# Low-rank, gate and head-sum products from float32r halves, and VectorE block transposes in the triangular solve of an RWKV-7 branch

## Chip, cores and metric

The kernel runs on one core of a Trainium2 chip. The metric is the device time of one execution in microseconds. One execution is one launch of the whole program; the median of three executions is compared.

## What is computed

One decoder layer in inference, for 256 prompt tokens and for 8 sample sequences of 8 tokens (320 columns together), with d_model 2048. Three branches (HGRN2, RWKV-7, short gated convolution) read one wide projection; gates merge them, an output projection and an MLP with 8192 hidden channels follow. All arrays are float32. The part that matters here is the RWKV-7 branch:

```python
xs = rw + (prev - rw) * rw_mu                      # token shift of the projected rows
r, kr, vr, wd, ad, gd = jnp.split(xs, cuts, axis=-1)
w_log = -jax.nn.softplus(-(rw_w0 + jnp.tanh(wd) @ rw_w2)) - 0.5   # low-rank, 64 wide
decay = jnp.exp(-jnp.exp(w_log))
a = jax.nn.sigmoid(rw_a0 + ad @ rw_a2)             # low-rank, 64 wide
g = jax.nn.sigmoid(gd) @ rw_g2                     # gate, 128 wide
kk = hs(kr * rw_k_k)
kk = kk / jnp.maximum(jnp.sqrt(jnp.sum(kk * kk, -1, keepdims=True)), 1e-12)  # head sum
k = kr * (1.0 + (a - 1.0) * rw_k_a)
# per token: S = S (diag(w) - kk^T (a kk)) + v^T k ;  o = S r
bonus = jnp.sum(r_ * k_ * rw_r_k, -1, keepdims=True) * v_                    # head sum
o_rw = (groupnorm(o_rw) + bonus) * g
```

There are 16 heads of 64 channels; the recurrence starts from zero for the prompt and from given states for the samples.

## The kernel before

Channels lie on the 128 partitions and the 320 columns along the free dimension. Every dense product takes weight granules of 8 blocks of 128x128: SyncE's queue loads a granule (`raw`), ScalarE casts it to float32r (`whi_t`, L104), VectorE subtracts to get the low part (`wlo_t`, L105), each in two pieces of 512 columns; then TensorE runs three matmuls per block, high by high (L128), high by low (L129) and low by high (L130). High and low parts have three buffers each.

The stages run in this order. First the input is loaded, normalised and split (`xh`, `xl`, L199 and L200). Then comes `rwkv` with the short convolution in it: projections RWA and RG give the low-rank inputs `L` and `Lg`; then there are 8 pairs of heads, j = 0 to 7. For each pair, `rwkv_front(j)` makes three projections through `shift_mix` (k, r, v), the two low-rank products from `L` (L346, contraction over 64 rows each, one on the lower and one on the upper partitions), the head sum of the squared keys with the block matrix `bo1` (L368) and its reciprocal root, the scaled operands LYR and BK, the transposed values (L396, L397), the head sum for the bonus (L407), and the transposes of BK (L415). `rwkv_solve(j)` forms the products of each chunk of 64 tokens (L441 and after), inverts I - N: the 16x16 diagonal blocks go through DRAM to a layout with one block on a partition, where VectorE runs a back substitution of 15 steps (L472, L474), and come back through DRAM as `Pm` (L477); then two doubling steps, h = 16 and h = 32, each need M, the transpose of P: four TensorE transposes of 128x128 (L497), a ScalarE copy to `Mm` (L498), four products with N (L501), a masked copy (L504), four products with P (L507) and an addition (L508). `rwkv_chunks(j)` runs the four chunks in order, then the samples, group norm, and the gate product from `lg` and `Lg` (L609). Outside the float32r granules these products are float32; the profile shows each float32 matmul of L346, L368, L407 and L609 as two records, a transpose as one.

The source order in the loop is solve(j+1), chunks(j), short convolution, front(j+2). The tile framework orders each engine's instructions when the program is compiled, by priorities in source order, dependencies, free buffers and its own estimate of the durations; every engine then runs its list in that order and waits at semaphores. So granule matmuls of later projections stand between the small products. Most working tiles of a pair come from a pool with one buffer (`wp`); tiles with one tag share a buffer.

After that follow HGRN2 with the merge of the convolution branch, the other merges, the output projection and the MLP, which the change does not touch.

Of the kernel before, what the change touches and what calls it, by code (L numbers as in the profile page):

```python
# [9 lines left out]
F32 = mybir.dt.float32  # L10
F32R = mybir.dt.float32r
# [5 lines left out]
# Columns of every feature-major tile: 256 prompt tokens, then 8 sample  # L17
# sequences of 8 tokens each.
# [8 lines left out]
# Tile indices (128 columns each) inside w_in.  # L27
# [5 lines left out]
# Columns of the packed per-channel parameters.  # L33
# [10 lines left out]
# words between two diagonal 16x16 blocks of a [128, 640] array  # L44
# [5 lines left out]
def _constants():  # L50
    """Identity, block matrices and masks: they depend on shapes alone."""
    r = np.arange(128)
    s, q = r[:, None], np.arange(64)[None, :]
    c = np.arange(NT)
    cols = {}
    cols["id"] = np.eye(128)
    cols["bo1"] = (r[:, None] // 64 == r[None, :] // 64)
    cols["bo64"] = cols["bo1"] / 64.0
    up, upi = (s % 64 < q), (s % 64 <= q)
    same = (s % 64) // 8 == q // 8  # L60
    cols["mkp"] = np.concatenate([up, upi, up], 1)
    cols["mks"] = np.concatenate([up & same, upi & same, up & same], 1)
    first = np.where(c < NP, c % 64 == 0, c % 8 == 0)[None, :] & np.ones((128, 1), bool)
    cols["m01"] = ~first
    cols["m10"] = first
    cols["mb"] = (s % 64) // 8 == np.arange(8)[None, :]
    for h in _LV:
        n = np.arange(64 // h)[None, :]
        cols["left%d" % h] = (s // (2 * h) == n) & (s % (2 * h) < h)
        if h in (16, 32):  # L70
            cols["right%d" % h] = (s // (2 * h) == n) & (s % (2 * h) >= h)
    cols["eye16"] = np.broadcast_to(np.eye(16).reshape(1, 256), (128, 256))
    off, parts, o = {}, [], 0
    for k, v in cols.items():
        off[k] = (o, v.shape[1])
        parts.append(np.broadcast_to(v, (128, v.shape[1])).astype(np.float32))
        o += v.shape[1]
    return off, np.ascontiguousarray(np.concatenate(parts, 1))
# [8 lines left out]
class K:  # L87
# [19 lines left out]
    def granule(self, src, pool=None):  # L107
        """8 weight blocks of 128x128 as float32r high and low parts."""
        raw = self.wraw.tile([128, 1024], F32, name="raw")
        self.nc.sync.dma_start(raw, src)  # L110
        hi = (pool or self.whi).tile([128, 1024], F32R, name="whi_t")
        lo = (pool or self.wlo).tile([128, 1024], F32R, name="wlo_t")
        for q in range(2):
            c = slice(512 * q, 512 * q + 512)
            self.split(hi[:, c], lo[:, c], raw[:, c])
        return hi, lo

    def dense(self, granules, ah, al):
        """PSUM tile = sum over the granules of weight block ^T @ activation block."""
        ps = self.mm.tile([128, 512], F32, name="mm_t")  # L120
        n = len(granules) * 8
        i = 0
        for g in granules:
            hi, lo = self.granule(g)
            for k in range(8):
                w = slice(k * 128, k * 128 + 128)
                mmul = self.nc.tensor.matmul
                mmul(ps[:, :NT], hi[:, w], ah[:, i, :], start=(i == 0), stop=False)  # L128
                mmul(ps[:, :NT], hi[:, w], al[:, i, :], start=False, stop=False)  # L129
                mmul(ps[:, :NT], lo[:, w], ah[:, i, :], start=False, stop=(i == n - 1))  # L130
                i += 1
        return ps[:, :NT]

    def dense_wide(self, tiles, ah, al, psp, wpool):
        """Several column tiles at once, one activation block after the other."""
# [19 lines left out]
    def rsqrt(self, pool, v, tag):  # L155
        """1/sqrt(v): table square root, reciprocal, one Newton step."""
        nc = self.nc
        shp = [128, NT]
        y = pool.tile(shp, F32, name=tag + "_y")
        t = pool.tile(shp, F32, name=tag + "_t")  # L160
        nc.scalar.activation(t, v, AF.Sqrt)
        nc.vector.reciprocal(y, t)
        nc.gpsimd.tensor_mul(t, y, y)
        nc.gpsimd.tensor_mul(t, t, v)
        nc.vector.tensor_scalar(t, t, -0.5, 1.5, ALU.mult, ALU.add)
        nc.vector.tensor_mul(y, y, t)
        return y

    # -----------------------------------------------------------------------
    def build(self):  # L170
# [9 lines left out]
        self.onesr = cp.tile([128, 128], F32R, name="onesr")  # L180
        nc.sync.dma_start(self.p, io["par"])
# [7 lines left out]
        with ExitStack() as cx:  # L189
# [6 lines left out]
            nc.sync.dma_start(self.c, io["cst"])  # L196
            for k in range(KD):
# [14 lines left out]
        # operands of the sample sequences' new states wait in DRAM  # L212
# [40 lines left out]
    def shift_mix(self, wp, n, name, packed):  # L253
        """Projected tile n with the token shift mixed in; keeps the last rows."""
# [22 lines left out]
    def rwkv(self, cx):  # L277
# [16 lines left out]
        # tiles whose constant blocks are written once  # L294
# [10 lines left out]
        # DRAM scratch through which the diagonal 16x16 blocks change layout  # L305
# [7 lines left out]
        self.L = kp.tile([128, NT], F32, name="L")  # L313
        nc.scalar.activation(self.L[0:64, :], xwa[0:64, :], AF.Tanh)
        nc.scalar.copy(self.L[64:128, :], xwa[64:128, :])
        xg = self.shift_mix(w2, RG, "v", True)
        self.Lg = kp.tile([128, NT], F32, name="Lg")
        nc.scalar.activation(self.Lg, xg, AF.Sigmoid)
# [13 lines left out]

    def rwkv_front(self, j, wp, w2):
# [9 lines left out]
        # decay, gate and rate from the low-rank projections  # L343
        def lora(lhsT, rhs):
            ps = self.pa.tile([128, 512], F32, name="pa_t")
            T.matmul(ps[:, :NT], lhsT, rhs, start=True, stop=True)  # L346
# [5 lines left out]
        S.activation(sg, lora(lw[0:64, :], self.L[0:64, :]), AF.Sigmoid, bias=self.par("w0", j))  # L352
        S.activation(a, lora(lw[64:128, :], self.L[64:128, :]), AF.Sigmoid, bias=self.par("a0", j))
# [10 lines left out]
        # normalised kk, k with its rate  # L364
# [3 lines left out]
        T.matmul(ss[:, :NT], self.cst("bo1"), sq, start=True, stop=True)  # L368
# [22 lines left out]
        # token-major values: X holds [state or u ; v] per chunk and head  # L391
# [15 lines left out]
        T.matmul(bs[:, :NT], self.cst("bo1"), rk, start=True, stop=True)  # L407
        V.tensor_mul(vx, bs[:, :NT], vx)

        # token-major [beta ; kappa]  # L410
# [10 lines left out]
    def rwkv_solve(self, j, front, wp):  # L421
# [7 lines left out]
        # pairwise products inside each chunk  # L429
        Nb = Z["Nb"].rearrange("p (c w) -> p c w", w=128)  # L430
        GB = Z["GB%d" % (j % 2)].rearrange("p (c h w) -> p c h w", h=2, w=64)
        for mk, cc in (("mkp", slice(0, 4)), ("mks", slice(4, 5))):
# [10 lines left out]
            for h, rows in ((0, lo), (1, hi)):  # L443
                p3 = pp[h]
                orow = hi if h == 0 else lo
                ca = lo if h == 0 else hi        # columns of alpha
                cr = hi if h == 0 else lo        # columns of rho
# [9 lines left out]
        # P = (I - N)^-1: diagonal 16x16 blocks first, each on one partition  # L457
# [21 lines left out]
        # then doubling, with M = P^T  # L479
        Pm = Z["Pm%d" % (j % 2)].rearrange("p (c w) -> p c w", w=128)  # L480
        Mm = Z["Mm"].rearrange("p (c w) -> p c w", w=128)
        blk = lambda i: slice(i * 128, i * 128 + 128)
# [10 lines left out]
        for h in (16, 32):  # L493
            T3 = Z["T%d" % h].rearrange("p (c w) -> p c w", w=128)
            ps = self.pinv.tile([128, 512], F32, name="pi")
            for i in range(4):
                T.transpose(ps[:, blk(i)], Pm[:, i, :], ident)  # L497
            S.copy(Z["Mm"], ps)  # L498
# [12 lines left out]
    def rwkv_chunks(self, j, front, wp, w2):  # L511
# [13 lines left out]
        # prompt chunks in order  # L525
# [34 lines left out]
        # the sample sequences: all states against all tokens, then select  # L560
# [31 lines left out]
        # group norm per head, bonus, gate  # L592
# [16 lines left out]
        T.matmul(gp[:, :NT], lg, self.Lg, start=True, stop=True)  # L609
        V.tensor_mul(self.B[:, j, :], gp[:, :NT], o)  # L610

    def rwkv_state(self, j, wp):
        """New states of the sample sequences for one pair of heads."""
# [58 lines left out]
    def hgrn(self, cx, filler):  # L672
# [7 lines left out]
        # lower bound of the forget gate: softmax over the layers, its  # L680
        # cumulative sum less the first row, clipped
# [20 lines left out]
    def hgrn_head(self, j, w1, w2):  # L702
# [28 lines left out]
        # token-major values  # L731
# [9 lines left out]
        # A[s, t]: blocks (s0,t0) (s1,t1) (s0,t1) sample  # L741
# [17 lines left out]
        for h in (1, 2, 4, 8, 16, 32, 64, 128):  # L759
# [23 lines left out]
            # extend to blocks of 2h  # L783
# [13 lines left out]
        # outputs  # L797
# [10 lines left out]
        # states  # L808
# [16 lines left out]
        # norm over the head, gate  # L825
# [15 lines left out]
    def hgrn_load(self, heads, wp):  # L841
        """Operands of the sample sequences' new states, for two heads each:
        values per sequence, old states with their decay."""
# [114 lines left out]
    def norm_from(self, sp, pp, acc, tag):  # L958
        """Broadcast 1/sqrt(mean + eps): tokens on partitions for the scalar
        steps, then spread again by a product with a diagonal matrix."""  # L960
# [98 lines left out]
def _layout(a):  # L1059
# [3 lines left out]
    # weight granules: [column tile, half, row in block, block, column]  # L1063
# [58 lines left out]
```

## Time and profile before

| What | Value |
|---|---|
| Runs | 2499.78, 2500.53 and 2504.2 us, median 2500.53 us |
| Profiled execution | span 2502.3 us (the page gives no other time of its own); 42443 instructions |
| TensorE matmul busy | 2456.1 us, 98% |
| VectorE busy | 1523.7 us, 61% |
| ScalarE busy | 980.0 us, 39% |
| GpSimd busy | 409.4 us, 16% |
| Mean granted TensorE clock | 0.992 |

The span runs from the first to the last instruction of the profiled execution. Busy times of matmuls are modelled at their ends, and matmuls overlap in the pipeline, so the distance from one start to the next is what a matmul costs in a stream. The RWKV stage with the short convolution lies between about 30 us and 600 us of the span.

### The profile page before, as it was taken

The page shows a single profiled execution, that of the slowest core. Times are in us where ns is not written, and L with a number is a line of the kernel's source. Part 1 is how long each engine was busy: PE and PEld are TensorE (multiplying, and loading weights), DVE is VectorE, ACT ScalarE, POOL GpSimd, SP SyncE. Part 2 cuts the span into 40 slices and gives each one's busy share as a digit, 9 for nine tenths or more (in the row PEclk, how much of TensorE's full clock was granted, in tenths as well). Part 3 has the DMA queues.
Part 4 walks back from the last instruction along what each step waited for, and adds up shares of the span by engine and source line. Part 5 has one row for each costly group of instructions (what it writes and reads, how often), then busy time and mean ns, then how long its engine had stood idle before and what let it go on. Part 6 is the DMA issues. An engine that isn't in the chain of part 4 may idle for free.

```text
span 2502.3 us, 42443 instructions
## 1 busy us (share of the span) xinstructions
PE 2456.1 (98%) x16588; PEld 2337.3 (93%) x16588; DVE 1523.7 (61%) x3022; ACT 980.0 (39%) x1882; POOL 409.4 (16%) x558
## 2 busy tenths in 40 slices
PE   8999999999999999999999999899999999999998
PEld 7887888889999999999999897899999999999997
DVE  6878888786565665565555445854555555555555
ACT  5433434433433333343444334434333333333333
POOL 5423333231000000011111233400000000000003
PEclk9999999999999999999999999899999999999999
DMA  6333333334434344344444655444444444444443
GB/s 215 120 84 89 99 112 122 115 124 127 138 129 137 129 137 131 127 143 148 151 152 147 214 189 184 131 149 151 152 148 150 149 152 152 147 149 151 152 150 129
DMA packets 131703, 355.02 MB, mean 142 GB/s; under 512 B 34864, under 2 KB 43440, under 8 KB 131504
## 3 DMA queue, kind: packets, MB, share of 16 engines
q1 hardware_dynamic: 131504, 352.32, 43.1%
q8 instruction: 131, 2.15, 0.4%
q14 instruction: 68, 0.56, 0.1%
HBM read 337.13 MB, written 15.14 MB: 141 GB/s over the span
## 4 chain that ended last, share of the span: by engine, by line
PE 89%; DVE 7%; POOL 1%; DMA 1%; issue 1%; SPq 0%; ACT 0%; POOLq 0%; DVEq 0%; ACTq 0%
PE mm_t L128 27%; PE mm_t L129 26%; PE mm_t L130 26%; DVE wlo_t L105 1%; PE pi L501 1%; DMA Pm<-dP 1%; PE pi L441 1%; PE pho_t L805 1%; PE plv_t L765 1%; DVE x L941 1%; PE pi L507 1%; PE plv_t L766 0%; DVE hl L943 0%; DVE xl L200 0%; PE po_t L550 0%
## 5 line engine op out<-in xcount | busy, mean ns | idle before, releaser
L104 ACT CAST whi_t<-raw 128x512 fp32r<-128x512 f32 x1192 | 685.1, 619 | 1159.5 <-PE mm_t L129 726.5
L105 DVE TENSOR_TENSOR wlo_t<-raw,whi_t 128x512 fp32r<-128x512 f32 x1192 | 831.5, 727 | 304.2 <-ACT whi_t L104 295.4
L130 PE MATMUL mm_t<-xh,wlo_t 128*128 128x320 f32 x2080 | 656.1, 316 | 1.8 <-DVE wlo_t L105 1.7
L128 PE MATMUL mm_t<-xh,whi_t 128*128 128x320 f32 x2080 | 657.4, 316 | 0.0
L129 PE MATMUL mm_t<-xl,whi_t 128*128 128x320 f32 x2080 | 655.6, 315 | 0.0
L130 PEld LDWEIGHTS mm_t<-xh,wlo_t 128*128 128x128 f32 x2080 | 392.5, 189 | 9.1 <-DVE wlo_t L105 3.0
L128 PEld LDWEIGHTS mm_t<-xh,whi_t 128*128 128x128 f32 x2080 | 392.8, 189 | 8.0 <-issue 0.9
L129 PEld LDWEIGHTS mm_t<-xl,whi_t 128*128 128x128 f32 x2080 | 393.2, 189 | 4.6 <-issue 0.4
L128 PE MATMUL mm_t<-hh,whi_t 128*128 128x320 f32 x1232 | 382.2, 310 | 0.0
L129 PE MATMUL mm_t<-hl,whi_t 128*128 128x320 f32 x1232 | 381.4, 310 | 0.0
L130 PE MATMUL mm_t<-hh,wlo_t 128*128 128x320 f32 x1232 | 381.3, 310 | 0.0
L130 PE MATMUL mm_t<-rh,wlo_t 128*128 128x320 f32 x1024 | 316.8, 309 | 0.0
L128 PE MATMUL mm_t<-rh,whi_t 128*128 128x320 f32 x1024 | 316.8, 309 | 0.0
L129 PE MATMUL mm_t<-rl,whi_t 128*128 128x320 f32 x1024 | 316.8, 309 | 0.0
L128 PEld LDWEIGHTS mm_t<-hh,whi_t 128*128 128x128 f32 x1232 | 231.9, 188 | 6.5 <-ACT sqt L955 4.9
L129 PEld LDWEIGHTS mm_t<-hl,whi_t 128*128 128x128 f32 x1232 | 231.9, 188 | 0.0
L130 PEld LDWEIGHTS mm_t<-hh,wlo_t 128*128 128x128 f32 x1232 | 231.9, 188 | 0.0
L130 PEld LDWEIGHTS mm_t<-rh,wlo_t 128*128 128x128 f32 x1024 | 192.3, 188 | 0.0
L128 PEld LDWEIGHTS mm_t<-rh,whi_t 128*128 128x128 f32 x1024 | 192.3, 188 | 0.0
L129 PEld LDWEIGHTS mm_t<-rl,whi_t 128*128 128x128 f32 x1024 | 192.3, 188 | 0.0
L1024 DVE TENSOR_TENSOR m<-m,mm_t 128x320 f32<-128x320 f32 x112 | 54.7, 488 | 189.4 <-PE mm_t L130 189.4
L956 POOL TENSOR_TENSOR ssf<-ssf,sqt 128x320 f32<-128x320 f32 x14 | 13.9, 993 | 841.7 <-issue 809.6
(410 smaller groups left out, 2762.0 us busy)
## 6 DMA issues: line engine op xcount, KB each, us to landing
raw<-w_in SPq DMA_DIRECT2D x260, 512.0 KB
raw<-w_ff SPq DMA_DIRECT2D x256, 512.0 KB
raw<-w_o SPq DMA_DIRECT2D x32, 512.0 KB
hs<-s_hg SPq DMA_DIRECT2D x16, 512.0 KB
raw<-w_pc SPq DMA_DIRECT2D x16, 512.0 KB
raw<-w_pb SPq DMA_DIRECT2D x16, 512.0 KB
raw<-w_pa SPq DMA_DIRECT2D x16, 512.0 KB
o_hgs<-hsn SPq DMA_DIRECT2D x16, 256.0 KB
```

What stands on the lines that cost most here:

```text
L104: self.nc.scalar.copy(hi, src)
L105: self.nc.vector.tensor_sub(lo, src, hi)
L128: mmul(ps[:, :NT], hi[:, w], ah[:, i, :], start=(i == 0), stop=False)
L129: mmul(ps[:, :NT], hi[:, w], al[:, i, :], start=False, stop=False)
L130: mmul(ps[:, :NT], lo[:, w], ah[:, i, :], start=False, stop=(i == n - 1))
L441: T.matmul(pp[h][:, i, :], BK[rows, c, h:h + 2, :].rearrange("p a w -> p (a w)"), LYR[rows, c, h].rearrange("p a w -> p (a w)"), start=Tru ...
L501: T.matmul(ps[:, half(i)], Nb[:, i, :], cols(Mm[:, i, :], h, 0), start=True, stop=True)
L507: T.matmul(ps[:, half(i)], T3[:, i, :], cols(Pm[:, i, :], h, 1), start=True, stop=True)
L765: T.matmul(ps[:, 0:64], KS[:, 0:128], rh[:, 0:hb], start=True, stop=True)
L805: T.matmul(op[:, 256:320], s0[:, b, :], QX[:, 64 * b:64 * b + 64], start=(b == 0), stop=False)
L941: nc.vector.scalar_tensor_tensor(x1, t, self.par("g2", k), x1, ALU.mult, ALU.add)
L1024: nc.vector.tensor_add(d, d, ps)
```

## The change

The low-rank products, the gate product and the two head sums take float32r operands. A new helper `halves` splits a float32 tile into a float32r high and low part (one ScalarE cast, one VectorE subtraction). `three` makes a product of two split operands by three matmuls; `head_sums` multiplies the block matrix, held once in float32r as `bor`, with both halves of its operand by two matmuls. `L` and `Lg` become pairs of halves; `tanh` and `sigmoid` are written in place before. The halves take buffers of existing tags: those of the squared keys share `tk` and `rkk`, those of the bonus operand share `sq` and `rn_t`; the halves of `lw` and of `lg` share the new tags `lwh` and `lwl`. In the solve, the four TensorE transposes and the ScalarE copy of each doubling step become one VectorE transpose of 32x32 blocks over 128x512. `bor` is made by a VectorE copy that stands in the source ahead of the loop that splits the input. The remaining lines of the diff take out comments and docstrings.

```diff
+        self.bor = cp.tile([128, 128], F32R, name="bor")
...
             nc.sync.dma_start(self.c, io["cst"])
+            nc.vector.tensor_copy(self.bor, self.cst("bo1"))
             for k in range(KD):
...
-        self.L = kp.tile([128, NT], F32, name="L")
-        nc.scalar.activation(self.L[0:64, :], xwa[0:64, :], AF.Tanh)
-        nc.scalar.copy(self.L[64:128, :], xwa[64:128, :])
+        nc.scalar.activation(xwa[0:64, :], xwa[0:64, :], AF.Tanh)
+        self.L = self.halves(kp, xwa, NT, "L")
         xg = self.shift_mix(w2, RG, "v", True)
-        self.Lg = kp.tile([128, NT], F32, name="Lg")
-        nc.scalar.activation(self.Lg, xg, AF.Sigmoid)
+        nc.scalar.activation(xg, xg, AF.Sigmoid)
+        self.Lg = self.halves(kp, xg, NT, "Lg")
...
+    def halves(self, pool, src, n, name, tags=None):
+        h = pool.tile([128, n], F32R, name=name + "h", tag=tags[0] if tags else name + "h")
+        l = pool.tile([128, n], F32R, name=name + "l", tag=tags[1] if tags else name + "l")
+        self.split(h, l, src)
+        return h, l
+    def three(self, out, w, x, rows=slice(0, 128)):
+        mmul = self.nc.tensor.matmul
+        mmul(out, w[0][rows], x[0][rows], start=True, stop=False)
+        mmul(out, w[0][rows], x[1][rows], start=False, stop=False)
+        mmul(out, w[1][rows], x[0][rows], start=False, stop=True)
+    def head_sums(self, out, wp, src, tags):
+        h, l = self.halves(wp, src, NT, "hs", tags)
+        self.nc.tensor.matmul(out, self.bor, h, start=True, stop=False)
+        self.nc.tensor.matmul(out, self.bor, l, start=False, stop=True)
...
-        def lora(lhsT, rhs):
+        lwr = self.halves(wp, lw, 128, "lw", ("lwh", "lwl"))
+        def lora(rows):
             ps = self.pa.tile([128, 512], F32, name="pa_t")
-            T.matmul(ps[:, :NT], lhsT, rhs, start=True, stop=True)
+            self.three(ps[:, :NT], lwr, self.L, rows)
...
-        T.matmul(ss[:, :NT], self.cst("bo1"), sq, start=True, stop=True)
+        self.head_sums(ss[:, :NT], wp, sq, ("tk", "rkk"))
...
-        T.matmul(bs[:, :NT], self.cst("bo1"), rk, start=True, stop=True)
+        self.head_sums(bs[:, :NT], wp, rk, ("sq", "rn_t"))
...
         for h in (16, 32):
-            ps = self.pinv.tile([128, 512], F32, name="pi")
-            for i in range(4):
-                T.transpose(ps[:, blk(i)], Pm[:, i, :], ident)
-            S.copy(Z["Mm"], ps)
+            V.transpose(Z["Mm"], Z["Pm%d" % (j % 2)][:, 0:512])
...
-        T.matmul(gp[:, :NT], lg, self.Lg, start=True, stop=True)
+        self.three(gp[:, :NT], self.halves(wp, lg, 128, "lg", ("lwh", "lwl")), self.Lg)
```

More of the change, by code (lines that the diff above doesn't have):

```diff
@@ L351, in rwkv_front @@
         G.tensor_copy(wt[:, 0:1], self.zero)
-        S.activation(sg, lora(lw[0:64, :], self.L[0:64, :]), AF.Sigmoid, bias=self.par("w0", j))
-        S.activation(a, lora(lw[64:128, :], self.L[64:128, :]), AF.Sigmoid, bias=self.par("a0", j))
+        S.activation(sg, lora(slice(0, 64)), AF.Sigmoid, bias=self.par("w0", j))
+        S.activation(a, lora(slice(64, 128)), AF.Sigmoid, bias=self.par("a0", j))
         S.activation(wt[:, 1:], sg, AF.Exp, scale=-EXP_MHALF)
@@ L481, in rwkv_solve @@
         Mm = Z["Mm"].rearrange("p (c w) -> p c w", w=128)
-        blk = lambda i: slice(i * 128, i * 128 + 128)
         half = lambda i: slice(i * 64, i * 64 + 64)
```

## The prediction

> **What bounds the kernel now.** I read the page's busy times first, then the stretches by stage, then what TensorE waited for in the RWKV stage, then the timeline around each edited instruction.
>
> ```profile
> span 2502.3 us, 42443 instructions
> ...
> PE 2456.1 (98%) x16588; PEld 2337.3 (93%) x16588; DVE 1523.7 (61%) x3022; ACT 980.0 (39%) x1882; POOL 409.4 (16%) x558
> ```
>
> ```profile
> 62.00:130.00 68.00, 62.28 (x420) 58.72 (x421) 53.91 (x125) 30.10 (x62) 28.58 (x45) 0.95 0.39 121
> 130.00:600.00 470.00, 456.86 (x3241) 395.69 (x3240) 369.24 (x899) 181.19 (x376) 148.44 (x267) 0.99 0.34 104
> 600.00:1000.00 400.00, 399.90 (x2763) 390.40 (x2762) 245.80 (x564) 160.82 (x308) 37.67 (x43) 1.00 0.43 138
> ```
>
> Columns of the second: stretch, its length, busy time of PE, PEld, DVE, ACT and POOL, granted clock, DMA. TensorE bounds the whole; from 600 us it never rests. The change lies almost wholly in the RWKV stage, 62 to 600 us, where TensorE rests 5.7 + 13.1 = 18.9 us and VectorE is busy 53.91 + 369.24 = 423 of 538 us, 79% against 61% over the span. So what TensorE no longer does is time gained, unless VectorE, which gets new work, makes TensorE wait.
>
> ```profile
> PE pa_t L396 <- DVE xsv L271: 6.7, 3, 2.5
> PE pi L497 <- DMA Pm<-dP: 3.5, 3, 1.3
> PE pa_t L415 <- DVE t L472: 3.5, 1, 3.5
> PE pa_t L415 <- DVE BK L386: 1.8, 1, 1.8
> ```
>
> ```profile
> 100.00:105.00 5.00, 1.55 (x14) 1.31 (x13) 4.94 (x18) 1.60 (x3) 1.07 (x3) 0.96 0.00 0
> 104.00:112.00 8.00, 7.49 (x43) 7.07 (x44) 5.77 (x20) 3.10 (x10) 4.57 (x5) 0.57 0.34 80
> ...
> 292.00:296.00 4.00, 1.52 (x8) 0.84 (x6) 3.99 (x9) 0.00 (x0) 2.69 (x3) 0.97 0.17 6
> 295.00:300.00 5.00, 4.19 (x19) 3.87 (x20) 5.00 (x7) 2.46 (x7) 2.44 (x6) 0.66 0.12 9
> ```
>
> Above: who waited for whom in 60 to 600 us (total, times, longest). The long waits end on VectorE: three before the value transposes (L396), two before the BK transposes (L415). The stretches show two of these places: VectorE is busy 4.94 of 5 and 3.99 of 4 us while TensorE works 1.5 us. Behind each stands a lowered clock: 0.57 over 8 us loses 3.4 us, 0.66 over 5 us loses 1.7 us.
>
> **The change, part by part.** What a matmul costs in the stream is the distance of starts:
>
> ```profile
> 169.07 0.31 PE L129 MATMUL mm_t<-xl,whi_t 128*128 128x320 f32 x1
> 169.31 0.80 PE L346 MATMUL pa_t<-L,lw 64*128 64x320 f32 x2
> 170.04 0.41 PE L130 MATMUL mm_t<-xh,wlo_t 128*128 128x320 f32 x1
> 170.29 0.31 PE L128 MATMUL mm_t<-xh,whi_t 128*128 128x320 f32 x1
> ...
> 304.63 0.31 PE L129 MATMUL mm_t<-xl,whi_t 128*128 128x320 f32 x1
> 304.78 0.70 PE L407 MATMUL pa_t<-rkk,c 128*128 128x320 f32 x2
> 305.31 0.60 PE L497 MATMUL pi<-c,Pm 128*128 128x128 f32 x4
> 305.67 0.39 PE L130 MATMUL mm_t<-xh,wlo_t 128*128 128x320 f32 x1
> 305.90 0.31 PE L128 MATMUL mm_t<-xh,whi_t 128*128 128x320 f32 x1
> ...
> 357.15 0.81 PE L346 MATMUL pa_t<-L,lw 64*128 64x320 f32 x4
> 357.89 0.33 PE L534 MATMUL py_t<-X,LYR 128*64 128x64 f32 x3
> ```
>
> ```profile
> L346 PE MATMUL pa_t<-L,lw 64*128 64x320 f32 x32 | 10.4, 481 | 0.0
> ...
> L497 PE MATMUL pi<-c,Pm 128*128 128x128 f32 x64 | 10.4, 287 | 3.5 <-DMA Pm<-dP 3.5
> ...
> L407 PE MATMUL pa_t<-rkk,c 128*128 128x320 f32 x16 | 6.0, 455 | 0.9 <-DVE rkk L389 0.9
> L368 PE MATMUL pa_t<-sq,c 128*128 128x320 f32 x16 | 5.9, 451 | 0.1
> ...
> L609 PE MATMUL pa_t<-Lg,lg 128*128 128x320 f32 x16 | 5.6, 433 | 0.0
> ```
>
> A float32r matmul of 320 columns takes 0.15 us (304.63 to 304.78, 0.147 over a longer stream); a float32 product of two records takes 0.53 (304.78 to 305.31); four transposes take 0.36 and delay the next matmul by 0.08 more (0.23 instead of 0.15).
>
> *Transposes.* 64 records are 16 groups of four: 16 x 0.44 = 7.0 us leave TensorE. Nothing covers this, since TensorE is the bound. Ends: 5.8 (no delay behind) and, with the rest before L497 (3.5 us) gone as well, 10.5. I take 7.0: the DMA of Pm is not made earlier, so that rest moves to the products with N (L501).
>
> *Head sums.* 32 records are 16 products. Two float32r matmuls instead of one float32 product save 0.53 - 0.29 = 0.24. A matmul that waits for fresh halves may have its weight load exposed:
>
> ```profile
> L834 PE MATMUL plv_t<-sqh,onesr x8: 413/415/417, 647.1 to 1064.8; 128*128 128x320 f32 x8
> ...
> L835 PE MATMUL plv_t<-sql,onesr x8: 308/310/312, 647.8 to 1065.5; 128*128 128x320 f32 x8
> ```
>
> This is the same construct in HGRN2, the first line 0.105 us longer. Ends 0.13 and 0.24, taken in the middle: 16 x 0.18 = 2.9 us.
>
> *Gate product.* 0.53 becomes 3 x 0.147 = 0.44: 8 x 0.09 = 0.7 us. With two exposed loads the lower end is -0.9; `lg` is there early, so I take 0.7.
>
> *Low-rank products.* Two records cost 0.92: from 169.07 to 170.29 is 1.22, less two granule matmuls. Each of the two passes (0.27 in L407) carries about 0.1 more, and so do the neighbours: with 64 rows no weight load hides. Three float32r matmuls carry that three times: 3 x (0.147 + 0.10) + 0.19 at the neighbours = 0.93. So 0 gained, though the arithmetic alone says 0.09 each. Where loads hid, 16 x (0.92 - 0.44) = 7.7 would be gained. At 357.15 the two products of a pair run side by side (four records in 0.74); three of the eight pairs do so, and three matmuls in a row might not: up to 3 x 0.93 = 2.8 lost. I take 0, the value of the isolated row.
> The Trainium skill, "TensorE: Matmul & The Clock Gate", Part 3, says that a weight load overlaps running matmuls only when the row group differs. By that rule these products gain nothing, as the row has it; without it the sum would be better by 7.7.
>
> *New VectorE and ScalarE work.*
>
> ```profile
> L498 ACT COPY Mm<-pi 128x512 f32<-128x512 f32 x16 | 9.4, 586 | 26.9 <-PE pi L497 26.8
> ...
> L105 DVE TENSOR_TENSOR sql<-hsq,sqh 128x320 fp32r<-128x320 f32 x8 | 3.9, 492 | 40.0 <-ACT sqh L104 40.0
> ...
> L104 ACT CAST sqh<-hsq 128x320 fp32r<-128x320 f32 x8 | 3.7, 459 | 0.2
> ```
>
> ```profile
> L188 DVE CAST onesr<-ones x1: 292/292/292, 1.0 to 1.0; 128x128 fp32r<-128x128 f32 x1
> ```
>
> ```profile
> L105 DVE TENSOR_TENSOR wlo_t<-raw,whi_t 128x512 fp32r<-128x512 f32 x178 | 123.3, 712 | 8.5 <-ACT whi_t L104 7.5
> ```
>
> No block transpose is in the trace. Its nearest row has the same shape on the same engine, 0.71 us; ends 0.3 (the rate of the 128x128 cast on a quarter of the elements) and 1.42 (two passes). Per pair VectorE gets 2 x 0.71, two subtractions of 0.49 and two of 128x128 at about 0.29: 3.0 us. Over 8 pairs, with `L`, `Lg` and `bor`, that is 25 us, 79% becomes 83%. ScalarE swaps two copies of 0.586 for two casts of 0.459 and two small ones: nothing, and it is two thirds idle.
> Where TensorE's waits end on VectorE this work is not hidden. Ahead of the three L396 waits stand the subtractions of `lw` and the squared keys: 3 x 0.78 = 2.3 us. The two L415 waits, in the fronts with no earlier pair's work beside them, get cast and subtraction of the squared keys in the chain plus the one of `lw`: 2 x 1.24 = 2.5 us. Elsewhere granules split ahead cover it; with that cover gone at every pair, 8 x 3.0 = 24 us is the worst. Ends 0 and 24; I take 4.8, since only these five places show VectorE as the last to finish.
> The shared tags make `tk` wait for the head sum and the second halves for the root; both are in the same chain and not late elsewhere. The halves of `lw` wait for the gate product of an earlier pair, which needs little room, since its halves can be made when `lg` lands.
>
> *The wait for Pm.* It moves from TensorE to VectorE's list. Behind it stand weight splits; TensorE lives meanwhile on granules split ahead. 0 taken; if TensorE meets the 3.5 us twice, -3.5.
>
> *The copy to `bor`.*
>
> ```profile
> 6.98 13.55 DVE L200 SCALAR_TENSOR_TENSOR xl<-x,p,xh 128x320 fp32r<-128x320 f32 x16 [5.66 <-ACT xh L199]
> ```
>
> ```profile
> 13.64 0.39 ACT L468 COPY Pd<-c 40x256 f32<-40x256 f32 x1
> ```
>
> It joins VectorE's opening list, which is the chain before the first granule matmuls: 0.3 us. The constants were there by 13.64; placed after the eighth subtraction the copy waits for nothing.
>
> **Sum.** 7.0 + 2.9 + 0.7 + 0 = 10.6 off TensorE, 4.8 + 0.3 = 5.1 back: 5.5 us. The profiled span lies 1.8 us above the median of the runs, 2500.53; I subtract from the median: 2495.0 us.
>
> **Rivals.** *Cover holds everywhere.* Only averages matter: 17% of VectorE stays free, and the 4.8 does not appear. For it: from 300 to 600 us hardly a wait on VectorE is seen, and every list is ordered anew. Gain 10.3: 2490.2, or less if a lowered clock goes too.
> *VectorE takes the gain back.* The waits above double (12 us instead of 6.7 + 3.5 + 1.8), or `bor` is put at the head of the list and holds the splits from 6.98 to 13.64, 6.7 us: about 10.6 - 10 = 0.6 gained, 2500.
> *Slower: a new long wait with a lowered clock.* One mechanism: 3 us more VectorE work in a pair makes one wait like that at 292 us (2.5 us), and the clock falls behind it (3.4 us as at 104). Each costs 5.9. Two eat the 10.6; three give 17.7 - 10.6 = 7.1 slower, 2507.6. Against it: TensorE gets less work in a pair too, 1.3 us.
> The Trainium skill, same page, Part 1, puts the gate's window at 3.4 us, free-running, so that shorter waits need not lower the clock. The trace has it lowered behind a wait of 2.5 us, too; by the page's rule the rival would need longer waits than I priced.
>
> **How the numbers follow.** The forecast, 3 to 8 us gained, has 0.45; full cover 0.24; gain taken back 0.17; slower 0.14. A measurement tells 0.2%, 5 us, from no change. Of the forecast's 0.45, 0.28 lies beyond 5 us: faster 0.28 + 0.24 = 0.52, same 0.17 + 0.17 = 0.34, slower 0.14. The range goes from 2487 (full cover, with one lowered clock of 3.4 gone) to 2505, halfway into the slower case; its forecast alone spans 2492 to 2498.
>
> **What would show it.** L497 and the copy to Mm gone, a VectorE transpose of 0.6 to 0.8 us sixteen times; head sums at 0.29 to 0.40 from start to start; three low-rank records in about 0.9; VectorE at 83% from 62 to 600 us; the stage's end earlier by the whole gain, nothing after it. Wrong would be: TensorE's rest in the stage well above 24 us or below 19, more or fewer stretches of lowered clock, transposes above 1.4 us, low-rank products at 0.45, or a first granule matmul later than before.

## The result, and the profile after

The changed kernel takes 2534.13 us (median of 4 runs, 2533.97 to 2535.69) against 2501.81 us before: ratio 1.0128, 95% interval 1.0114 to 1.0143. It is 32 us slower; the forecast was 2495.0 us, range 2487 to 2505.

The head of the page of after:

```profile
span 2532.2 us, 42457 instructions
...
PE 2468.3 (97%) x16548; PEld 2356.5 (93%) x16548; DVE 1537.5 (61%) x3073; ACT 980.9 (39%) x1898; POOL 411.1 (16%) x558
```

The span is 29.9 us longer, yet TensorE has 40 records fewer and its busy time grew by 12. Matmuls that take longer without being more mean a lower clock. The stretches of after (columns as in the prediction: stretch, length, PE, PEld, DVE, ACT, POOL, clock, DMA) say where:

```profile
62.00:130.00 68.00, 57.85 (x390) 54.43 (x389) 54.06 (x129) 29.73 (x62) 27.72 (x45) 0.90 0.35 112
130.00:600.00 470.00, 442.29 (x3000) 391.34 (x2999) 364.14 (x901) 171.82 (x368) 146.22 (x255) 0.92 0.31 100
600.00:1000.00 400.00, 399.75 (x2765) 386.69 (x2764) 246.50 (x556) 159.62 (x307) 41.91 (x52) 1.00 0.39 135
```

From 130 to 600 us the granted clock is 0.92 instead of 0.99, TensorE rests 27.7 us instead of 13.1, and it starts 241 matmuls fewer. From 600 us on all is as before. The last product into `pa_t` starts at 622.1 us instead of 592.1, so the whole loss lies in the RWKV stage. Who waited for whom there (60 to 600 us: total, times, longest):

```profile
PE pa_t L351 <- ACT hsh L104: 11.7, 6, 4.9
PE pi L521 <- DVE Mm L518: 9.0, 6, 3.7
PE mm_t L128 <- DVE sh L671: 3.3, 2, 3.1
PE pa_t L351 <- DVE B L630: 2.4, 1, 2.4
```

None of these was among the long waits of before. The second, closely: TensorE, then VectorE (start, duration, what; in brackets the idle time before it and its releaser).

```profile
180.38 0.31 PE L129 MATMUL mm_t<-xl,whi_t 128*128 128x320 f32 x1
184.38 1.97 PE L521 MATMUL pi<-Mm,Nb 128*128 128x64 f32 x8 [3.69 <-DVE Mm L518]
186.86 1.97 PE L527 MATMUL pi<-Pm,T 128*128 128x64 f32 x8 [0.52 <-DVE T L524]
188.59 0.61 PE L351 MATMUL pa_t<-hsh,bor 128*128 128x320 f32 x1
```

```profile
175.61 2.14 DVE L385 RECIPROCAL Wi<-W 128x320 f32<-128x320 f32 x1
177.67 2.09 DVE L162 RECIPROCAL rn_y<-rn_t 128x320 f32<-128x320 f32 x1
...
180.68 1.14 DVE L406 TENSOR_TENSOR tk<-tk,xsk 128x320 f32<-128x320 f32 x1
...
183.61 0.71 DVE L518 STREAM_TRANSPOSE Mm<-Pm 128x512 f32<-128x512 f32 x1
```

The transpose itself takes 0.71 us, but it stands behind two reciprocals and much other work of the next pair's front, and TensorE has nothing but the solve next in its list: no granule matmul stands between L521 and L527. What happened to the clock (stretches of 3.4 us, TensorE alone: length, busy time, records, clock), first all matmuls, then the granule matmuls alone:

```profile
180.00:183.40 3.40, 0.69 (x5) 1.00 0.37 82
```

```profile
183.60:187.00 3.40, 2.11 (x9) 0.50 0.00 0
190.40:193.80 3.40, 3.40 (x17) 0.50 0.35 126
197.30:200.70 3.40, 3.40 (x18) 0.50 0.02 5
204.10:207.50 3.40, 3.40 (x12) 0.50 0.11 42
214.30:217.70 3.40, 3.40 (x19) 0.50 0.19 72
217.70:221.10 3.40, 3.40 (x27) 0.99 0.40 154
```

```profile
190.40:193.80 3.40, 0.27 (x1) 0.50 0.35 126
197.30:200.70 3.40, 0.00 (x0) 0.50 0.02 5
204.10:207.50 3.40, 2.52 (x9) 0.50 0.11 42
214.30:217.70 3.40, 2.50 (x9) 0.50 0.19 72
```

The clock fell after 3.4 us with 0.69 us of work, and then stayed at 0.50 for 34.1 us, though by the trace TensorE was busy without a gap from 190.4 to 207.5 us: at first with products of 64 columns and hardly a granule. It came back only after granule matmuls had filled more than half of four stretches in a row. The Trainium skill, "TensorE: Matmul & The Clock Gate", Part 1, has the clock fall after an idle window of about 3.4 us and return after one busy window of that length. The fall comes near this; the return does not, since 17 busy us did not bring it. What decides is not settled here: nine granule matmuls stand in the stretch at 204.10 as in that at 214.30.

### The profile page after: what moved, and what is told of

Read it like the earlier page. It is cut to its first block, busy times and chain, and to the rows that moved or that the text cites. A ratio compares the mean times of both kernels' runs of the same rounds, so it can differ in the third digit from the quotient of the medians.

```text
span 2532.2 us, 42457 instructions
## 1 busy us (share of the span) xinstructions
PE 2468.3 (97%) x16548; PEld 2356.5 (93%) x16548; DVE 1537.5 (61%) x3073; ACT 980.9 (39%) x1898; POOL 411.1 (16%) x558
## 4 chain that ended last, share of the span: by engine, by line
PE 88%; DVE 8%; POOL 2%; DMA 1%; issue 1%; ACT 0%; SPq 0%; DVEq 0%; POOLq 0%; ACTq 0%
PE mm_t L128 26%; PE mm_t L129 26%; PE mm_t L130 26%; DVE wlo_t L105 1%; PE pi L464 1%; PE pi L521 1%; PE pi L527 1%; DMA Pm<-dP 1%; PE pho_t L825 1%; PE plv_t L785 1%; DVE x L961 1%; PE plv_t L786 0%; DVE rn_y L162 0%; DVE hl L963 0%; DVE xl L202 0%
```

## The experiments

Times at the lowered clock below are summed from the trace's clock records up to 640 us: 17.1 us before, 92.2 after. Each kernel has one trace; those of e6 and e8 are of the shortest of four executions (2513.3 and 2525.9 us, medians 2518.07 and 2535.15). "Stage end" is the start of the last product into `pa_t`: 592.1 before, 622.1 after. Comparisons are with runs of before on the same chip, medians 2502.6 to 2502.9.

Theories at the start: T, the transposes in VectorE's list are late and TensorE waits; H, the split head sums make waits; later L (as T, with the clock falling where only small products follow), W (less TensorE work lowers the clock) and S (what loses is the new order of all lists, which the tile framework makes when it compiles; it is called the planner here).

**Which part.** e1 is before with this edit alone, e2 is after with it undone.

```diff
-            ps = self.pinv.tile([128, 512], F32, name="pi")
-            for i in range(4):
-                T.transpose(ps[:, blk(i)], Pm[:, i, :], ident)
-            S.copy(Z["Mm"], ps)
+            V.transpose(Z["Mm"], Z["Pm%d" % (j % 2)][:, 0:512])
```

> Kernel before with one part of the change: the solve's transposes by VectorE, all products as before. Theory T (the transposes stand in VectorE's list behind other work, TensorE's products with N wait for them up to 4 us and the clock falls behind those waits): slower than before by 12 to 25 us, 2514 to 2527, with most of the stretches of lowered clock of the changed kernel. Theory H (the split head sums make the waits): this part alone takes 7 us off TensorE and gives little back, 2494 to 2499. Rival S (every change of the list moves waits about, whichever part): anything, with waits at places that neither part touches.

> Changed kernel with the transposes back on TensorE and the copy to Mm on ScalarE; all products from float32r halves. Theory T: near before or faster, 2494 to 2503, since 4 us leave TensorE and the waits for Mm are gone. Theory H: slower than before by 12 to 25 us, 2514 to 2527, with TensorE waiting 10 us or more for the cast of the bonus operand (hsh). If both parts cost, each loses 10 to 20 us.

e1: 2530.53 us, ratio 1.0113 (1.0096 to 1.013), 81.9 us at the lowered clock. e2: 2521.76 us, 1.0073 (1.0058 to 1.0088), 61.4 us. Each part loses alone, e1 3 us beyond T's range, e2 within H's. But 28 + 19 is more than 32, so something common may be counted twice. In e1 the head sums are untouched and the longest wait is T's:

```profile
PE pi L498 <- DVE Mm L495: 11.5, 7, 2.5
```

**The halves' buffers, and the bonus sum.** e3 and e4 are after with one line changed:

```diff
-        self.head_sums(bs[:, :NT], wp, rk, ("sq", "rn_t"))
+        self.head_sums(bs[:, :NT], wp, rk, ("sg", "wt"))                          # e3
+        T.matmul(bs[:, :NT], self.cst("bo1"), rk, start=True, stop=True)          # e4
```

> Changed kernel, but the halves of the bonus operand take the buffers of sg and wt, which come free after the scan, instead of sq and rn_t, which come free only after the reciprocal root. If the shared buffers make the bonus head sum late, TensorE's wait for hsh (11.7 us in the changed kernel) falls under 4 us and the time to 2505 to 2520. If not, 2530 to 2537 and the wait stays.

> Changed kernel with the bonus head sum as one float32 product again; the rest as changed. Theory H: the wait for hsh and its lowered clock go, 2508 to 2520. Theory T: 2530 to 2538, since the waits for Mm stay (and 0.24 us per pair go back to TensorE).

e3: 2530.86 us, 1.011 (1.0095 to 1.0125). e4: 2532.95 us, 1.0123 (1.0107 to 1.0138). Neither is the cause; the waits only changed place. In e3 the wait for `hsh` (L351) falls from 11.7 to 4.6 us, and the one for the second half (L352) becomes 5.0. In e4 the head sum's is no longer among the longest, and the solve's has grown from 9.0:

```profile
PE pi L521 <- DVE Mm L518: 12.6, 8, 4.7
```

**Edits that change no work.** e5 moves the copy to Mm to VectorE (`V.tensor_copy`), e6 swaps the two low-rank lines of the source, e6b puts the three lines of the bonus product behind the BK transposes. All are made in the kernel before.

```diff
-            S.copy(Z["Mm"], ps)
+            V.tensor_copy(Z["Mm"], ps)                                     # e5
...
-        S.activation(sg, lora(lw[0:64, :], self.L[0:64, :]), AF.Sigmoid, bias=self.par("w0", j))
         S.activation(a, lora(lw[64:128, :], self.L[64:128, :]), AF.Sigmoid, bias=self.par("a0", j))
+        S.activation(sg, lora(lw[0:64, :], self.L[0:64, :]), AF.Sigmoid, bias=self.par("w0", j))   # e6
```

> Kernel before, with the copy of the transposes to Mm done by VectorE instead of ScalarE; all TensorE work as before. Theory L (a step of the solve that stands in VectorE's list comes late, TensorE waits for it in front of the small products of the solve, the clock falls there and stays low through them): slower by 10 to 25 us, 2512 to 2528, with waits of the products with N (L501) for a VectorE Mm and 50 us or more at the low clock before 640 us, against 17 in the kernel before. Theory W (the loss comes from the transposes being gone from TensorE's work): as before, 2499 to 2506.

> Kernel before with the two low-rank products in the other source order: the same instructions, another order of the lists. Rival S (the list of the kernel before is a lucky one and any other order loses): slower by 8 to 25 us, 2511 to 2528, with 40 to 80 us at the low clock before 640 us. Theory L: within 5 us of before, 2498 to 2508.

> Kernel before with the bonus head sum behind the BK transposes in the source: the same instructions, another order of the lists. Rival S: slower by 8 to 25 us, 2511 to 2528. Theory L: within 5 us of before, 2498 to 2508.

e5: 2518.89 us, 1.0064 (1.0049 to 1.0079), 44.4 us at the lowered clock. e6: 2518.07 us, 1.0066 (1.0042 to 1.0089), 34.1 us. e6b: 2522.23 us, 1.0079 (1.0064 to 1.0094), 54.6 us. e6 and e6b run the very instructions of before in another order and lose 16 and 20 us. So S is real, though e6's time at the lowered clock lies below S's 40 to 80 us, and the loss of e2 is no larger than that of a neutral edit. e5's time lies in L's range, but not by L's mechanism: no product with N (L501) waits for `Mm` there, and the longest wait is that of the bonus head sum:

```profile
PE pa_t L407 <- DVE rkk L389: 6.1, 3, 3.5
```

**Is it the missing TensorE work?** e8: before with Mm from the VectorE transpose, while TensorE still makes its four transposes into a tile that nobody reads.

```diff
-            S.copy(Z["Mm"], ps)
+            V.transpose(Z["Mm"], Z["Pm%d" % (j % 2)][:, 0:512])
```

> Kernel before with Mm made by VectorE's block transpose, while TensorE still makes its four transposes per step, whose result is not read. Theory L: as slow as with the transposes gone, 2525 to 2540, since Mm still stands in VectorE's list (and 7 us of TensorE work are kept). Theory W: as before, 2499 to 2508, since TensorE's work keeps the clock up.

e8: 2535.15 us, 1.013 (1.0114 to 1.0147). W falls: TensorE has all its work, and the loss is as large as that of the whole change. L has the time right and the wait wrong: TensorE waits only 2.1 us for `Mm` (L501), and 6.8 us for Pm to land ahead of the transposes that nobody reads.

All nine kernels to which the planner gave a new order (after, e1 to e6b, e8) lose, by 15 to 33 us.

**The order held.** The remaining kernels fix the order of every engine's list. At the end of the build each instruction is told to issue behind the one that precedes it in a stored list, without a wait. `traced` are the instructions in the order of the program's text, `at` is the next place of one engine's list.

```diff
+    info = mybir.DependencyInfo(mybir.DependencyClass.NoSync, mybir.DependencyReason.DATA)
...
+            at += d + 1
+            if last is not None:
+                tc.add_manual_dep(traced[at], traced[last].name, info, reason="order")
+            last = at
```

In the order of before, the edit's new instructions stand where the operand was ready in the profile of before, and products stand where the replaced ones stood.

> The kernel before with the solve's transposes on VectorE, and every engine's list held in the order of the kernel before (issue order only, no added wait): nothing moves but the 64 TensorE transposes and 16 ScalarE copies that go, and the 16 VectorE transposes, each put ahead of the first VectorE instruction that started after the first of its four TensorE transposes in the profile of before. If the loss comes from new orders (theory S), the clock's lowered time before 640 us stays near the 17.1 us of before (below 30), and the time is 2490 to 2502: the 7 us that the transposes' TensorE time was worth, less up to a VectorE instruction's wait (0.7 to 2 us) at a few of the 16. If a transpose in VectorE's list is late wherever it stands (theory T, L), TensorE waits 2 to 4 us ahead of L521 in some of the 16 steps, over 40 us run at the lowered clock and the time is 2512 or more, about the 12 us by which the kernels with VectorE transposes lay above those without.

e9: 2503.73 us, 1.0004 (0.9995 to 1.0013), 27.3 us at the lowered clock, stage end 593.7. The 27 us that e1 loses beyond this are order, which includes the places of the transposes in VectorE's list. But nothing is gained either: the time is 1.7 us above S's range and even with before. From 62 to 620 us (columns as above), before and e9:

```profile
62.00:620.00 558.00, 539.04 (x3792) 474.04 (x3793) 440.97 (x1066) 223.34 (x462) 182.42 (x318) 0.98 0.36 109
```

```profile
62.00:620.00 558.00, 533.53 (x3716) 468.81 (x3715) 447.15 (x1079) 213.65 (x443) 180.82 (x317) 0.98 0.36 108
```

TensorE works 5.5 us less and rests 5.5 us more. Most of the new rest has one address, in place of the 3.5 us before L497; the bonus head sum's wait (L407) grows from 0.9 to 2.2 us:

```profile
PE pi L498 <- DVE Mm L495: 6.7, 6, 3.3
```

**The halves with the order held.** For the bonus sum the shared tags `sq` and `rn_t` exclude before's order (there the bonus product comes ahead of the root of the squared keys), so it stays float32; the halves of `lg` share the tag `YA` and have one of their own.

> The float32r halves alone (low-rank, gate and squared-key head sum; the bonus head sum stays float32, since its shared buffers would forbid the order), with TensorE's transposes, every list in the order of the kernel before; the new casts and subtractions stand where their source was ready in the profile of before. Theory S: 2496 to 2502, since nothing moves and the products save 8 x 0.18 (head sums), 8 x 0.09 (gate) and 16 x 0.09 (low-rank) = 3.6 us at most. Theory H (the extra casts and subtractions ahead of the products make waits of themselves): 2510 or more, as the 2521.8 us of the halves in their own order.

> The whole change but the bonus head sum, every list in the order of the kernel before. Theory S: the gains of the two add up, 2486 to 2500 us, faster than before, against 2532.95 us for the same instructions in the order that the planner gave them: then all of the loss is order. Theories T, L: 2512 or more, with over 40 us at the lowered clock before 640 us.

e10: 2519.55 us, 1.0066 (1.0053 to 1.008). e11: 2517.84 us, 1.0065 (1.0051 to 1.008). What ran is not what the text expected: by an error in the stored list, most low-rank matmuls stood where the head sum belonged, so `a` came late:

```profile
PE pa_t L351 <- ACT a L376: 9.7, 3, 3.4
```

By accident they show that misplacing some 40 matmuls costs 9 to 13 us, against the next two kernels, which have the lists as intended.

> e10 with its mistake mended: halves for low-rank, gate and squared-key head sum at the places of the products that they replace, transposes on TensorE. S: 2496 to 2503 (nothing moves, up to 3.6 us of TensorE time saved, a few tenths of waits for the new casts). H: 2510 or more, near the 2521.8 us of the halves in the planner's order.

> In e10 and e11 the order was not held: five of the six low-rank matmuls of each tile had been put where the squared-key head sum stood in TensorE's list, so the second sigmoid came some 6 us late and TensorE waited for it. Here each group of three, and each pair of halves, stands exactly where the float32 product that it replaces stood; else as e11 (whole change but the bonus head sum, every other list in the order of the kernel before). Order theory S: 2495 to 2503, that is the 2503.7 us of the transposes alone in this order less up to 3.6 us for the products, against 2532.95 us in the planner's order. If the halves cost by themselves (H): 2510 or more.

e13 (halves): 2506.8 us, 1.0016 (1.0007 to 1.0025), clock as before (17.1 us). e12 (both): 2508.38 us, 1.0021 (1.0013 to 1.003), 37.5 us. Both lie 4 to 5 us above S's bounds, and 3 and 2 us below H's. e4 has e12's instructions, but for the buffers of `lg`, in the planner's order: 2532.95 - 2508.38 = 24.6 us are order. What is left against before, 5.8 us, is again waits; in e13 the one before the value transposes has grown from 6.7 us and three times to

```profile
PE pa_t L419 <- DVE xsv L273: 9.5, 4, 3.1
```

VectorE begins the `xsv` of the three places of before 0.5, 1.1 and 2.0 us later. The subtractions that now stand ahead of it may be why; no run takes them out.

**The mirror.** Every instruction of before in the order that the planner gave e1, the TensorE transposes up to eight granule matmuls ahead of their use.

> The mirror: the instructions of the kernel before, every one, in the order that the planner gave the kernel with VectorE transposes (e1); the four TensorE transposes stand up to 8 matmuls ahead of the products that need them, the ScalarE copy where the VectorE transpose had run. S: the order alone makes the loss, 2520 to 2540, with over 50 us at the lowered clock before 640 us, though no instruction is changed. If the transposes on VectorE, not the order, make the extra loss over a neutral reordering: 2515 to 2521, like the swapped low-rank products (2518.1).

e14: 2539.07 us, 1.0142 (1.0119 to 1.0165). No instruction of before is changed, and 36.5 us are lost, no less than in e1. The intervals of the two overlap, so the 2539.07 - 2530.53 = 8.5 us between them are not a measure of the transposes. The waits moved to the landing of Pm and the ScalarE copy:

```profile
PE pi L497 <- DMA Pm<-dP: 10.0, 4, 3.1
PE pi L501 <- ACT Mm L498: 5.9, 7, 1.7
```

The first stands ahead of the TensorE transposes, whose places were chosen for this kernel and not by the planner; part of e14's loss may be theirs. e6 and e6b have no such choice in them.

What the two orders differ in can be read from the built lists. Granule matmuls between the four products with N and the four with P, for the 16 doubling steps:

```text
before 8 5  2 7  3 4  7 3  11 6  4 13  1 7  5 9     none: 0 of 16
after  9 5  0 4  0 3 14 5   2 5  5 14  0 4  7 5     none: 3
e1     7 5  0 0  0 0  6 0   1 4  3  1  1 2  5 7     none: 5
e14    7 5  0 0  0 0  6 0   1 4  3  1  1 2  5 7     none: 5
```

Where nothing stands between, TensorE waits for VectorE's masked copy (0.52 us before L527 above), and only 64-column products run. This goes with the longest stretches at half clock: in the ten traces with a new order (e14's among them), 11 of the 12 stretches of over 20 us hold such a step, and the kernels in before's order have neither. But 16 of the 31 such steps lie outside these stretches, so a step of this kind does not always bring one, and no run changed the granules between these products alone.

**Two tries at a version faster than before.** e15 is e12 with this; e16: before in its own order, with three groups of value transposes moved behind the next 13, 10 and 17 granule matmuls; e17: e9 with the same moves.

```diff
+            if j < 6:
                 V.transpose(Z["Mm"], Z["Pm%d" % (j % 2)][:, 0:512])
+            else:
+                ps = self.pinv.tile([128, 512], F32, name="pi")
+                for i in range(4):
+                    T.transpose(ps[:, i * 128:i * 128 + 128], Pm[:, i, :], ident)
+                S.copy(Z["Mm"], ps)
```

> A version to beat both: as e12, but VectorE transposes only for tiles j below 6; the last two tiles, where e9 showed waits of 3.3 and 1.7 us ahead of L498, keep TensorE's. S: 2503.7 less 5.0 for those waits, 3.4 for the lowered clock at 492.9 us, 3.6 for the halves, plus 4 x 0.57 for the transposes that stay: 2494, range 2489 to 2500. If the halves cost by themselves: above 2505.

> The kernel before, its own order held, but for three places in TensorE's list: the three vx transposes (L396, L397) of tiles 2, 3 and 4 stand 13, 10 and 17 granule matmuls later (0.147 us each), so that these fill the waits of 1.92, 2.31 and 2.48 us for xsv that the profile of before shows at 176.6, 237.9 and 295.5 us; one ScalarE copy moves by one place with them. If waits in front of such steps cost by the time and by the lowered clock (S with the clock): up to 6.7 us of waits and half of the 10.2 us at the lowered clock go, 2491 to 2498. If VectorE sets the stage whatever TensorE's list is (rival), the waits come back at the next step for VectorE: 2500 to 2504.

> The same three moves in e9 (transposes on VectorE, order of before held). If the waits are what ate e9's gain: 2492 to 2499, below e9's 2503.7. If VectorE sets the stage: 2501 to 2506, since VectorE carries 16 x 0.7 us more.

e15: 2509.94 us, 1.0024 (1.0015 to 1.0032). e16: 2502.85 us, 0.9999 (0.999 to 1.0008). e17: 2508.22 us, 1.0019 (1.0011 to 1.0028). None beats before. e15 misses its range by 10 us, e17 lies above both of its ranges, e16 is where its rival had it; at before's time, it gives no sign that holding the order costs anything by itself. e16 filled the three waits for `xsv`, and they came back at the next things that VectorE delivers, low parts of granules and the emptying of a result:

```profile
PE mm_t L130 <- DVE wlo_t L105: 3.4, 3, 1.8
PE mm_t L128 <- DVE sb L666: 3.2, 1, 3.2
```

So with this order VectorE's chain sets these three stretches; other work for TensorE there did not help.

## Why the prediction was wrong

**The step that failed** is "4.8, since only these five places show VectorE as the last to finish". It took the waits of before as fixed places that get longer. The edit changes what the planner sees, so all lists came out anew, and the long waits of after stand at places where before had none. From 62 us to the stage's end (598 and 628 us) TensorE rests 37.9 us instead of 18.9, so 19 us more where 4.8 were taken, and 75 us more pass at half clock. I had written "every list is ordered anew", but only in favour of the best case. With the order held (e12) the step fails in a smaller way: it left out the wait for `Mm` (L521, 5.1 us) and had the one for `xsv` about right (9.4 us against 6.7 before, with 2.3 added).

**The size of a lowered clock** was the second error. I priced 3.4 us of loss per wait, the most seen in before. There granule matmuls followed soon behind the long waits (10 to 15 while the clock was low), and it was back after 6.8 us at most. In after one wait of 3.7 us was followed by 34.1 us at half clock, another place by 23.9. The slower rival had new waits with a lowered clock, at 5.9 us each and 2507.6 us in all, but put them down to more work for VectorE; e6 and e6b give it none and lose 16 and 20 us.

**TensorE's savings** were right or too small. Transposes: 7.0 us predicted. In e9 the stage ends 1.6 us later with 25.5 - 19.8 = 5.7 us more rest (30 to 640 us), so at least 5.7 - 1.6 = 4.1 us of work went. It also has 10.2 us more at half clock; if TensorE lost half of that, 5.1, it is 9.2 us. The 7.0 lies between these two estimates. Head sums: 0.13 to 0.24 gained each, taken as 0.18; with the halves ready it is the upper end (e13):

```profile
173.81 0.31 PE L351 MATMUL pa_t<-hsh,bor 128*128 128x320 f32 x1
173.96 0.31 PE L352 MATMUL pa_t<-hsl,bor 128*128 128x320 f32 x1
174.11 0.31 PE L130 MATMUL mm_t<-xh,wlo_t 128*128 128x320 f32 x1
```

Two starts in 0.30 us. Where TensorE has waited, the first takes 0.25 us instead of 0.15, the 0.1 of the lower end (after):

```profile
174.36 0.42 PE L351 MATMUL pa_t<-hsh,bor 128*128 128x320 f32 x1 [2.40 <-DVE B L630]
174.61 0.31 PE L352 MATMUL pa_t<-hsl,bor 128*128 128x320 f32 x1
```

Low-rank products: 0 predicted, from three exposed weight loads. In after, first the matmuls, then the weight loads (PEld):

```profile
237.40 0.31 PE L130 MATMUL mm_t<-xh,wlo_t 128*128 128x320 f32 x1
237.64 0.41 PE L344 MATMUL pa_t<-Lh,lwh 64*128 64x320 f32 x1
237.89 0.30 PE L345 MATMUL pa_t<-Ll,lwh 64*128 64x320 f32 x1
238.03 0.31 PE L346 MATMUL pa_t<-Lh,lwl 64*128 64x320 f32 x1
238.27 0.41 PE L128 MATMUL mm_t<-xh,whi_t 128*128 128x320 f32 x1
238.52 0.31 PE L129 MATMUL mm_t<-xl,whi_t 128*128 128x320 f32 x1
```

```profile
237.64 0.18 PEld L344 LDWEIGHTS pa_t<-Lh,lwh 64*128 64x128 f32 x1 [0.19 <-issue]
237.74 0.19 PEld L345 LDWEIGHTS pa_t<-Ll,lwh 64*128 64x128 f32 x1
237.89 0.18 PEld L346 LDWEIGHTS pa_t<-Lh,lwl 64*128 64x128 f32 x1
238.27 0.19 PEld L128 LDWEIGHTS mm_t<-xh,whi_t 128*128 128x128 f32 x1 [0.19 <-issue]
```

From 237.40 to 238.52 is 1.12 us; less two granule matmuls, 0.83, against 0.92 before. So 0.09 is gained each, 1.4 us in all: the arithmetic alone was right. The prediction put 0.1 us on every pass of 64 rows. The rows put it only where the product changes from 128 rows to 64 and back: there the load starts no sooner than its matmul (237.64, 238.27), and the steps around it are 0.24 and 0.25 us. The third matmul brings new weights and starts 0.14 us after the second; its load (237.89) runs beside that one. These two changes cost the same before and after. The rule of the Trainium skill weighed there ("TensorE: Matmul & The Clock Gate", Part 3), that a load overlaps running matmuls only when the row group differs, does not agree: the loads of L345 and L346 overlap matmuls on the same 64 rows.

**VectorE's new work** was sized well: 0.71 us for the transpose (row below), 0.48 for a subtraction, and the new records add up to 25.7 us against 25. Its share of 62 to 628 us was 77%, not 83%: the stage got longer, and VectorE's busy time in it grew by only 12.9 us, since records overlap and others got shorter. A share below 80% said nothing: e16 shows VectorE deciding the waits at that share.

```profile
L518 DVE STREAM_TRANSPOSE Mm<-Pm 128x512 f32<-128x512 f32 x16 | 11.3, 707 | 3.6 <-DMA Pm<-dP 3.6
```

The copy to `bor` delayed nothing, as assumed: the first granule matmul starts at 18.8 us, before at 19.7.

**What stays open.** The mirror was made for e1's order, not for that of the whole change; that 25 us of its 32 are order rests on e4 against e12, which have the bonus head sum in float32. With halves that sum never ran in before's order. Why before's order is better than all nine new ones, and why the planner puts fewer granules between the doubling steps, is not shown.

## What to carry to other kernels

When a planner orders the lists, an edit is priced twice: once by its instructions, once by the new order. A neutral edit of the source measures the second (here 16 to 20 us, three times what the first promised), and holding the old order measures the first alone. Before pricing a wait, look at what stands behind it in TensorE's list: in before, with granule matmuls soon behind it, a wait of 2.5 us was followed by 3.4 us at half clock; in after, ahead of a chain of small products, one of 3.7 us was followed by 34.1 us. If TensorE's rests end on one other engine's list, work taken from TensorE can come back as rest, however far below full that engine's share is.

## What the runs showed of the hardware

The clock stayed at half for 34.1 us in which TensorE, by the trace, was busy almost throughout after the first 7 us, at first with products of 64 columns; being busy for 17 us was not enough to raise it. Where float32r matmuls change from 128 to 64 rows and back, the weight load is not hidden behind a running matmul: the change costs about 0.2 us each way (0.24 and 0.25 us from start to start instead of twice 0.15). Between matmuls on the same 64 rows it is hidden, also where it brings new weights (0.14 us). A VectorE transpose of 128x512 float32 in 32x32 blocks takes 0.71 us, the same as a subtraction of that shape.
